# Long convolution spread over projection and FFN units, FFN units dealt out anew, some FFN weights of the third chunk kept split in HBM

## The chip, the cores and the metric

The kernel runs on 1 core of one Trainium2 chip. The metric is the device time of one launch in microseconds; three runs before the change took 2460.94 to 2464.22 us, with a median of 2463.81 us. The engines are PE (TensorE, matrix products), DVE (VectorE), ACT (ScalarE), POOL (GpSimd) and SP (SyncE, which here only issues DMAs; POOL issues some too). Each engine takes its instructions in the order in which the program holds them.

## The reference

One layer of a streaming encoder in float32, width 1024, on 2048 prompt tokens and on 8 sequences of 16 sample tokens with histories of their own:

```
u = rms_norm(x, norm_mix) @ w_in          # 2564 columns: z, xBC, dt, q, k, v, short conv, conformer
ya = SSD(z, xBC, dt)                      # 4-tap conv, silu, chunked state-space scan, gated rms norm
yb = attention(q, k, v)                   # window of 128 positions in chunks of 64, ALiBi, sinks
yc = b * conv3(c * h)
yd = silu(layer_norm(conv31(a * sigmoid(g))))     # the long convolution: 31 taps, 256 channels
x = x + concat[ya, yb, yc, yd] @ w_out
x = x + (silu(hf @ w_gate) * (hf @ w_up)) @ w_down    # hf = rms_norm(x, norm_ffn), D_FF = 2816
y = rms_norm(x, norm_final)
```

All states (SSD, convolution histories, keys and values) are outputs too.

## The kernel before, in words

**Chunks.** Tokens lie along the free axis, features along the 128 partitions. `Cfg.chunks = (2, 4, 4, 3, 3)` makes five chunks c0 to c4 of 256, 512, 512, 512 (384 of the prompt and the 128 sample tokens) and 384 columns. The FFN of c0, c1 and c2 runs by units as below; that of c3 and c4 is done in a last phase in another form (`prep`, `gate2`, `up2`, then down).

**Units.** A unit is one weight tile and its products: `proj_in` has 21 (one for each name of `W_IN_TILES`: c, h, b for the short convolution, k, v, q, B, C, dt, x, z for attention and SSD, g and a for the long convolution), `proj_out` 8, and `ffn` 22 `gate`, 22 `up_` and some `down` units. In `down(j0, n, m2)` n hidden tiles from j0 on meet two output tiles; `rounds` deals the 22 hidden tiles out, (4,4,4,4,3,3) in c0 and c1 and `rounds_last` = (4,4,4,4,1,3,2) in c2. A full unit is 24 matmuls: `group` (lines 227 to 234) multiplies a high and a low part of the weights with a high and a low part of the operand, three products for each of 8 tiles.

**Weights.** `load_w` (line 208) loads a 512 KB tile into one of two `fr` buffers from SP's queue, and `split_w` (line 199) splits it into one of three `w` buffers: ACT copies the high part (line 201), DVE subtracts it for the low part (line 181). These run ahead of their unit, as far as buffers allow. Tiles with a key can be kept: in the first three chunks a third each of the 29 projection tiles (`key % 3 == ci`) is stored to HBM in its split form (1 MB, from POOL's queue, line 222), and later chunks load that straight into a `w` buffer (line 215), without ACT and DVE.

**Order.** `weave` writes the order out: it runs a list of units, and after given units it advances side work, pieces of generators that are spread evenly from one unit to another: norms, final outputs, and `mixers(c)`, which holds attention (`attend_prompt`, `attend_sample`), SSD blocks (`ssd`), the long convolution in eight pieces of up to eight taps (`conf_conv`), and the ends (`short`, `end_conf`, `end_ssd` and the attention output), which write the eight operand tiles of `proj_out` into the pool `act`. With `early` the list has all blocks of attention and SSD first and the convolution behind; `c["blocks"]` is the number of the former. A scheduler turns the order into one instruction order per engine.

**Buffers that matter here.** `act` has 16 buffers: 8 normalised tiles for `proj_in`, 8 operand tiles for `proj_out` or the FFN (`hf`); in c3 the sample attention and SSD need four of them for caches and states. `raw` has 2: an input of a convolution with its history in front; chunk 3 also loads sample histories into it and stores new ones from it (line 390). `mix` has 4, `b2` 4, `nt` 3 (x tiles, squares). Products go to four PSUM buffers, `pm`.

**The last chunks.** After `proj_out(c2)` the units of `proj_in(c3)`, in the order `FIRST` (g and a last), are merged with c2's first 18 FFN units, and 23 more follow. Then come `proj_out(c3)`, 3 FFN units, `proj_in(c4)` merged with 5, 9 more; then `proj_out(c4)` and 6, and 8 `down` units. `norm2(c2)` makes the hf tiles near the start of c3's list, `norm1(c4)` the operands of chunk 4, `stats2` the row norms of c3 and c4 for the last phase, and `prep` its operands in four rounds. In `proj_out` of c3 and c4 an x tile is loaded (line 841), the product added, and the sum stored to `mid` (line 847).

Of the kernel before, what the change touches and what calls it, by code (L numbers as in the profile page):

```python
# [17 lines left out]
P = 128  # L18
# [22 lines left out]
FIRST = ("B", "C", "x0", "x1", "dt", "k", "v", "q0", "q1", "c0", "h0", "b0", "c1", "h1", "b1", "z0", "z1",  # L41
         "g0", "a0", "g1", "a1")

EARLY = 11
# [71 lines left out]
def stream_step(ctx: ExitStack, tc: tile.TileContext, cfg, x, w_in, w_out, w_gu, w_down, tab, con, dist_p, dist_s,  # L116
# [87 lines left out]


    kept = {}

    def load_w(src, shape, key=None, ci=0):
        n = int(np.prod(shape))
        pat = {2: lambda v: v.rearrange("p (a b) -> p a b", b=shape[-1]),  # L210
               3: lambda v: v.rearrange("p (a b c) -> p a b c", b=shape[1], c=shape[2])}[len(shape)]
        with tc.high_priority(offset=AHEAD):
            if key in kept:
                d = mk(wp, [P, 2, 1024], "w", F32R, bufs=B["w"])
                sync.dma_start(d.bitcast(F32), kept[key])
            else:
                raw = mk(wp, [P, 1024], "fr", bufs=B["fr"])
                sync.dma_start(pat(raw[:, :n]), src)
                d = split_w(raw[:, :n], n)
        if key is not None and key not in kept and key % 3 == ci:  # L220
            kept[key] = dp.tile([P, 2, 1024], F32, tag=f"kept{key}", name=f"kept{key}")
            pool.dma_start(kept[key], d.bitcast(F32))
        return pat(d[:, 0, :n]), pat(d[:, 1, :n])

    tail = [None]
# [595 lines left out]
    def proj_in(c, names):  # L821
        c.setdefault("u", {})

        def unit(name):
            wh, wl = load_w(w_in[W_IN_TILES.index(name)], [KT, P], W_IN_TILES.index(name), c["i"])
            ps = mk(pm, [P, 512], "pm")
            group(ps, c["T"], [(wh[:, k], wl[:, k], c["xn"][k]) for k in range(KT)])
            after_in(c, name, ps)
# [3 lines left out]
    def proj_out(c):  # L832
# [3 lines left out]
        def unit(m):  # L836
# [4 lines left out]
            sync.dma_start(x2[:, :T], x[:, m, o:o + T])  # L841
            wh, wl = load_w(w_out[m], [KT, P], len(W_IN_TILES) + m, c["i"])
            ps = mk(pm, [P, 512], "pm")
# [28 lines left out]
    def ffn(c):  # L872
# [5 lines left out]
        def gate(j):  # L878
            wh, wl = load_w(w_gu[j, 0], [KT, P])
            ps = mk(pm, [P, 512], "pm")  # L880
# [5 lines left out]
        def up_(j):  # L886
            wh, wl = load_w(w_gu[j, 1], [KT, P])
            ps = mk(pm, [P, 512], "pm")
# [7 lines left out]
        def down(j0, n, m2, final):  # L896
            wh, wl = load_w(w_down[:, 2 * m2:2 * m2 + 2, j0:j0 + n], [2, n, P])
            for i in range(2):
# [53 lines left out]
    def twice(g, n=2):  # L952
        return [g] * n
# [25 lines left out]
    for c, nxt, after in ((c0, c1, c2), (c1, c2, c3)):  # L979
# [6 lines left out]

    weave(proj_out(c2), (twice(final(c1)), 0, 2), (twice(norm1(c3)), 0, 3))
    f = ffn(c2)
    s3 = proj_in(c3, FIRST)
    units = s3[:3] + merge(s3[3:], f[:18]) + f[18:41]  # L990
    m3 = mixers(c3, True)
    nb = c3["blocks"]
    weave(units, (twice(norm2(c2)), 0, 2), (m3[:nb], units.index(s3[8]) + 1, units.index(s3[-1]) + 6),
          (m3[nb:], units.index(s3[-1]) + 1, len(units) - 1),
          (twice(norm1_stats(c4)), 20, 35))
    s4 = proj_in(c4, FIRST)
    units = proj_out(c3) + f[41:44] + merge(s4, f[44:49]) + f[49:58]
    m4 = mixers(c4, True)
    nb = c4["blocks"]
    weave(units, ([stats2(c3)], 8, 9), (twice(norm1(c4)), 8, 11), (m4[:nb], units.index(s4[8]) + 1, units.index(s4[-1])), (m4[nb:], units.index(s4[-1]) + 1, len(units) - 1))  # L1000

# [157 lines left out]

    weave(proj_out(c4) + f[58:64], ([stats2(c4)], 8, 9), (prepared[:2], 9, 13))  # L1160
    operands.close()
# [226 lines left out]
```

## Time and profile before

| | |
|---|---|
| time of the profiled execution, its span | 2461.09 us, 2459.3 us |
| median of three runs | 2463.81 us |
| busy: PE, DVE, ACT, POOL | 2367.5, 1589.3, 876.7, 130.8 us |
| mean granted clock of TensorE | 0.987 |
| moved by DMA | 393.77 MB, mean 160 GB/s |
| splits of weight tiles (ACT line 201, DVE line 181) | 375 each |
| loads of kept tiles, stores of them | 88, 29 |

"Busy" is the time in which an engine had at least one instruction running. Matmuls overlap, so PE's busy time holds stretches in which it runs slowly. The granted clock is the share of full speed that the chip allowed TensorE. A view by stretches gives the busy time of each engine between two moments, counted from the start of the span; a view of waits gives who waited for whom, in us in total, times, and the longest.

### The profile page before, as it was taken

How to read it: one execution, taken by the hardware profiler on the slowest of the kernel's cores; microseconds unless marked ns; L12 is line 12 of the kernel's file. 1: busy time of each engine (PE TensorE's matmuls, PEld its weight loads, DVE VectorE, ACT ScalarE, POOL GpSimd, SP SyncE). 2: the span in 40 equal slices, each digit the busy share in tenths (PEclk: the TensorE clock that was granted, in tenths of full speed). 3: DMA queues.
4: the chain of work that ended last, by engine and by line, in shares of the span. 5: the costliest groups of instructions: out<-in, count | busy, mean ns of one | idle time of the engine just before them, and what ended most of it. 6: DMA issues, size and time to landing. Idle time of an engine off the chain costs nothing.

```text
span 2459.3 us, 32394 instructions
## 1 busy us (share of the span) xinstructions
PE 2367.5 (96%) x12443; PEld 2052.3 (83%) x12443; DVE 1589.3 (65%) x2997; ACT 876.7 (36%) x1461; POOL 130.8 (5%) x240
## 2 busy tenths in 40 slices
PE   6899999999999999989999999998889999999997
PEld 5788999878888888877887788987868999999997
DVE  6897998765784546556248963558497676663324
ACT  4534455423333233224112431332244444443221
POOL 0100000010000000010000000000001000000000
PEclk9999999999999999999999999999889999999998
DMA  7657445576422222466443136643533323338663
GB/s 250 247 174 271 138 155 163 197 266 248 146 89 87 91 90 78 153 248 174 148 143 128 62 103 235 219 164 112 192 112 116 127 92 120 124 117 300 213 195 118
DMA packets 130746, 393.77 MB, mean 160 GB/s; under 512 B 12464, under 2 KB 50256, under 8 KB 115616
## 3 DMA queue, kind: packets, MB, share of 16 engines
q1 hardware_dynamic: 116560, 327.20, 40.4%
q0 software_dynamic: 14032, 64.51, 7.1%
q8 instruction: 98, 1.61, 0.3%
q14 instruction: 56, 0.46, 0.1%
HBM read 326.69 MB, written 64.97 MB: 159 GB/s over the span
## 4 chain that ended last, share of the span: by engine, by line
PE 44%; issue 6%; DVE 3%; DMA 2%; ACT 0%; POOL 0%; DVEq 0%; SPq 0%; POOLq 0%; ACTq 0%
PE pm L1102 6%; PE pm L1103 6%; PE pm L1104 6%; PE pm L231 6%; PE pm L232 6%; PE pm L233 6%; PE px L1103 1%; PE px L1102 1%; PE px L1104 1%; DMA nt<-x 1%; DVE w L181 1%; DVE x L184 0%; DMA o_xc_s<-raw 0%; DMA act<-kc 0%; PE px L655 0%
## 5 line engine op out<-in xcount | busy, mean ns | idle before, releaser
L231 PE MATMUL pm<-act,w 128*128 128x512 f32 (+2 forms) x2216 | 804.2, 364 | 16.6 <-DMA w<-kept 7.0
L233 PE MATMUL pm<-act,w 128*128 128x512 f32 (+2 forms) x2216 | 796.8, 360 | 5.2 <-DVE w L181 5.1
L232 PE MATMUL pm<-act,w 128*128 128x512 f32 (+2 forms) x2216 | 795.8, 359 | 1.4 <-DVE act L181 1.4
L201 ACT ACTIVATE w<-fr 128x1024 fp32r<-128x1024 f32 (+3 forms) x375 | 388.3, 1036 | 892.9 <-PE pm L233 524.1
L181 DVE TENSOR_TENSOR w<-fr,w 128x1024 fp32r<-128x1024 f32 (+3 forms) x375 | 448.4, 1196 | 288.3 <-ACT w L201 287.0
L231 PEld LDWEIGHTS pm<-act,w 128*128 128x128 f32 x2216 | 420.2, 190 | 85.2 <-issue 9.4
L233 PEld LDWEIGHTS pm<-act,w 128*128 128x128 f32 x2216 | 420.3, 190 | 64.6 <-DVE w L181 7.5
L232 PEld LDWEIGHTS pm<-act,w 128*128 128x128 f32 x2216 | 420.6, 190 | 59.4 <-DVE act L181 2.3
L1102 PE MATMUL pm<-hf,w 128*128 128x448 f32 x616 | 225.6, 366 | 0.8 <-ACT g L1116 0.6
L1103 PE MATMUL pm<-hf,w 128*128 128x448 f32 x616 | 224.8, 365 | 0.0
L1104 PE MATMUL pm<-hf,w 128*128 128x448 f32 x616 | 223.8, 363 | 0.0
L231 PE MATMUL pm<-h,w 128*128 128x512 f32 (+1 forms) x528 | 192.3, 365 | 19.6 <-DVE x L181 12.9
L184 DVE SCALAR_TENSOR_TENSOR mix<-raw,tabh,mix 128x384 f32<-128x384 f32 (+3 forms) x360 | 199.9, 594 | 1.8
L232 PE MATMUL pm<-h,w 128*128 128x512 f32 (+1 forms) x528 | 189.2, 359 | 0.0
L233 PE MATMUL pm<-h,w 128*128 128x512 f32 (+1 forms) x528 | 188.3, 357 | 0.0
L181 DVE TENSOR_TENSOR x<-x,pm 128x512 f32<-128x512 f32 (+2 forms) x184 | 107.6, 600 | 67.4 <-PE pm L233 55.1
L231 PEld LDWEIGHTS pm<-h,w 128*128 128x128 f32 x528 | 100.3, 190 | 41.1 <-issue 12.3
L184 DVE SCALAR_TENSOR_TENSOR ft<-ft,pm 128x512 f32<-128x512 f32 (+1 forms) x132 | 78.7, 596 | 84.2 <-PE pm L233 67.2
L1102 PEld LDWEIGHTS pm<-hf,w 128*128 128x128 f32 x616 | 115.6, 188 | 10.6 <-ACT g L1116 1.0
L1104 PEld LDWEIGHTS pm<-hf,w 128*128 128x128 f32 x616 | 115.7, 188 | 9.4
L1103 PEld LDWEIGHTS pm<-hf,w 128*128 128x128 f32 x616 | 115.7, 188 | 8.2
L233 PEld LDWEIGHTS pm<-h,w 128*128 128x128 f32 x528 | 100.4, 190 | 15.2
(283 smaller groups left out, 2572.8 us busy)
## 6 DMA issues: line engine op xcount, KB each, us to landing
w<-kept SPq DMA_DIRECT2D x88, 1024.0 KB, 5.5
fr<-w_gu SPq DMA_DIRECT2D x176, 512.0 KB, 3.3
fr<-w_down SPq DMA_DIRECT2D x92, 512.0 KB, 3.7
kept<-w POOLq DMA_DIRECT2D x29, 1024.0 KB, 6.6
fr<-w_in SPq DMA_DIRECT2D x42, 512.0 KB, 4.3
hm<-h POOLq DMA_DIRECT2D x44, 448.0 KB, 4.4
ht<-hm SPq DMA_DIRECT2D x40, 448.0 KB, 5.2
nt<-x SPq DMA_DIRECT2D x56, 256.0 KB, 5.6
```

The costliest lines, as they stand in the source:

```text
L181: return eng.tensor_tensor(out=out, in0=a, in1=b, op=op)
L184: return eng.scalar_tensor_tensor(out=out, in0=a, scalar=s, in1=b, op0=op0, op1=op1)
L201: act.activation(d[:, 0, :n], raw, AF.Copy)
L231: pe.matmul(ps[:, :T], wh, o[:, 0, :T], start=(i == 0), stop=False)
L232: pe.matmul(ps[:, :T], wh, o[:, 1, :T], start=False, stop=False)
L233: mm = pe.matmul(ps[:, :T], wl, o[:, 0, :T], start=False, stop=(i == n - 1))
L1102: pe.matmul(ps[:, :N], wh[:, i], a, start=first and i == 0, stop=False, skip_group_check=True)
L1103: pe.matmul(ps[:, :N], wh[:, i], b, start=False, stop=False, skip_group_check=True)
L1104: mm = pe.matmul(ps[:, :N], wl[:, i], a, start=False, stop=(i == n - 1), skip_group_check=True)
```

## The change

The projection tiles are stored in chunks 1 and 2 only: even ones in chunk 1, the rest in chunk 2. Half of the FFN tiles (gates with even j, ups with odd j, down tiles with even m2) are stored in chunk 1's FFN and looked up by key in chunk 2's. In c3 and c4, `proj_in` runs in the order `SPREAD`, with g0 and a0 first and g1 and a1 in the middle; the pieces of the first convolution are spread from a0 to a1, those of the second, and `short`, from a1 to eight units before the end, the attention and SSD blocks from q1 to two units behind z1, and the ends of the mixers over the last seven units. c2's FFN units are dealt out anew over the three lists, and the norms around `proj_out(c2)` and the first rounds of `prep` are spaced differently.

```diff
+SPREAD = ("g0", "a0", "B", "C", "x0", "x1", "dt", "k", "v", "q0", "q1", "g1", "a1", "c0", "h0", "b0", "c1", "h1", "b1",
+          "z0", "z1")
...
-    def load_w(src, shape, key=None, ci=0):
+    def load_w(src, shape, key=None, store=False):
...
-                sync.dma_start(d.bitcast(F32), kept[key])
+                sync.dma_start(d[:, :, :n].bitcast(F32), kept[key])
...
-        if key is not None and key not in kept and key % 3 == ci:
-            kept[key] = dp.tile([P, 2, 1024], F32, tag=f"kept{key}", name=f"kept{key}")
-            pool.dma_start(kept[key], d.bitcast(F32))
+        if store and key not in kept:
+            uid[0] += 1
+            kept[key] = dp.tile([P, 2, n], F32, tag=f"kept{uid[0]}", name=f"kept{uid[0]}")
+            pool.dma_start(kept[key], d[:, :, :n].bitcast(F32))
         return pat(d[:, 0, :n]), pat(d[:, 1, :n])
+
+    def keep(c, n):
+        return c["i"] in (1, 2) and (c["i"] == 2 or n % 2 == 0)
...
-            wh, wl = load_w(w_in[W_IN_TILES.index(name)], [KT, P], W_IN_TILES.index(name), c["i"])
+            wh, wl = load_w(w_in[W_IN_TILES.index(name)], [KT, P], W_IN_TILES.index(name), keep(c, W_IN_TILES.index(name)))
...
-            wh, wl = load_w(w_out[m], [KT, P], len(W_IN_TILES) + m, c["i"])
+            wh, wl = load_w(w_out[m], [KT, P], len(W_IN_TILES) + m, keep(c, m))
...
-            wh, wl = load_w(w_gu[j, 0], [KT, P])
+            wh, wl = load_w(w_gu[j, 0], [KT, P], ("gu", j, 0), c["i"] == 1 and j % 2 == 0)
...
-            wh, wl = load_w(w_gu[j, 1], [KT, P])
+            wh, wl = load_w(w_gu[j, 1], [KT, P], ("gu", j, 1), c["i"] == 1 and j % 2 == 1)
...
-            wh, wl = load_w(w_down[:, 2 * m2:2 * m2 + 2, j0:j0 + n], [2, n, P])
+            wh, wl = load_w(w_down[:, 2 * m2:2 * m2 + 2, j0:j0 + n], [2, n, P], ("down", m2, j0, n),
+                            c["i"] == 1 and m2 % 2 == 0)
...
-    weave(proj_out(c2), (twice(final(c1)), 0, 2), (twice(norm1(c3)), 0, 3))
+    weave(proj_out(c2), (twice(final(c1)), 0, 4), (twice(norm1(c3)), 1, 5))
     f = ffn(c2)
-    s3 = proj_in(c3, FIRST)
-    units = s3[:3] + merge(s3[3:], f[:18]) + f[18:41]
-    m3 = mixers(c3, True)
-    nb = c3["blocks"]
-    weave(units, (twice(norm2(c2)), 0, 2), (m3[:nb], units.index(s3[8]) + 1, units.index(s3[-1]) + 6),
-          (m3[nb:], units.index(s3[-1]) + 1, len(units) - 1),
-          (twice(norm1_stats(c4)), 20, 35))
-    s4 = proj_in(c4, FIRST)
-    units = proj_out(c3) + f[41:44] + merge(s4, f[44:49]) + f[49:58]
-    m4 = mixers(c4, True)
-    nb = c4["blocks"]
-    weave(units, ([stats2(c3)], 8, 9), (twice(norm1(c4)), 8, 11), (m4[:nb], units.index(s4[8]) + 1, units.index(s4[-1])), (m4[nb:], units.index(s4[-1]) + 1, len(units) - 1))
+    def beside(c, s, units, end):
+
+        st = mixers(c, True)
+        at = {n: units.index(u) + 1 for n, u in zip(SPREAD, s)}
+        n = c["blocks"]
+        assert at["z1"] <= end - 7
+        return [(st[n:n + 4], at["a0"], at["a1"] - 1), (st[:n], at["q1"], min(at["z1"] + 2, end - 8)),
+                (st[n + 4:n + 9], at["a1"], end - 8), (st[n + 9:], end - 7, end)]
+
+    s3 = proj_in(c3, SPREAD)
+    units = s3[:3] + merge(s3[3:], f[:26]) + f[26:36]
+    weave(units, (twice(norm2(c2)), 0, 2), *beside(c3, s3, units, len(units) - 1), (twice(norm1_stats(c4)), 20, 35))
+    s4 = proj_in(c4, SPREAD)
+    units = proj_out(c3) + f[36:39] + merge(s4, f[39:44]) + f[44:53]
+    weave(units, ([stats2(c3)], 8, 9), (twice(norm1(c4)), 8, 11), *beside(c4, s4, units, len(units) - 1))
...
-    weave(proj_out(c4) + f[58:64], ([stats2(c4)], 8, 9), (prepared[:2], 9, 13))
+    weave(proj_out(c4) + f[53:64], ([stats2(c4)], 8, 9), (prepared[:2], 10, 17))
```

## The prediction

> **What bounds the kernel now.** I read the page's busy line and clock line first, then the waits of PE, then the busy time stretch by stretch, with the stretches cut where the stages of the code change.
>
> ```profile
> PE 2367.5 (96%) x12443; PEld 2052.3 (83%) x12443; DVE 1589.3 (65%) x2997; ACT 876.7 (36%) x1461; POOL 130.8 (5%) x240
> PEclk9999999999999999999999999999889999999998
> ```
>
> PE is the bound nearly everywhere, and the change leaves its number of matmuls as it is. So what can be won or lost is the time in which PE stands, or runs at a lower granted clock. The digits fall to 8 in slices 29 and 30, with PE still in the nineties: that loss does not show as idle time. The stretches show where it lies (columns: length, busy of PE, weight loads, DVE, ACT, POOL with counts, granted clock, DMA share, GB/s):
>
> ```profile
> core 0: us, PE busy (x) PEld busy (x) DVE busy (x) ACT busy (x) POOL busy (x), PEclk, DMA share, GB/s
> 18.00:109.00 91.00, 77.10 (x566) 71.34 (x567) 67.96 (x158) 44.61 (x87) 8.31 (x17) 0.98 0.71 252
> 109.00:177.00 68.00, 67.95 (x326) 54.69 (x326) 64.24 (x168) 24.56 (x52) 4.37 (x6) 1.00 0.57 194
> 644.00:1035.00 391.00, 391.00 (x1819) 316.69 (x1818) 237.12 (x402) 127.35 (x209) 8.95 (x16) 1.00 0.29 92
> 1085.00:1160.00 75.00, 67.11 (x295) 54.55 (x294) 51.75 (x110) 29.20 (x51) 8.70 (x11) 0.98 0.55 154
> 1160.00:1306.00 146.00, 146.00 (x639) 119.83 (x638) 61.00 (x119) 24.26 (x33) 6.19 (x9) 1.00 0.45 149
> 1306.00:1396.00 90.00, 87.71 (x555) 67.22 (x556) 75.02 (x218) 40.40 (x95) 7.37 (x20) 0.96 0.27 89
> 1396.00:1481.00 85.00, 85.00 (x388) 69.72 (x387) 61.47 (x120) 25.52 (x36) 0.00 (x0) 1.00 0.30 99
> 1543.00:1678.00 135.00, 133.62 (x775) 121.39 (x774) 73.42 (x173) 46.32 (x104) 9.32 (x22) 1.00 0.55 188
> 1678.00:1723.00 45.00, 35.75 (x145) 28.40 (x144) 43.35 (x79) 6.57 (x10) 0.54 (x1) 0.89 0.30 103
> 1723.00:1771.00 48.00, 42.47 (x220) 40.15 (x219) 19.54 (x51) 9.73 (x18) 2.70 (x5) 0.86 0.52 189
> 1771.00:1788.50 17.50, 15.35 (x73) 12.61 (x71) 9.39 (x23) 5.42 (x8) 1.62 (x3) 0.90 0.51 173
> 1788.50:1811.00 22.50, 22.50 (x101) 18.45 (x101) 21.97 (x36) 11.82 (x20) 0.00 (x0) 1.00 0.43 132
> 1811.00:1851.00 40.00, 31.77 (x121) 24.18 (x120) 37.49 (x63) 17.22 (x30) 0.00 (x0) 0.87 0.28 87
> ```
>
> Loss of a stretch = its length minus PE busy, plus (1 − clock) × PE busy. It is 15.4 us in 18 to 109 (chunk 0's projection), 9.2 in 1085 to 1160 (start of chunk 3's), 5.8 in 1306 to 1396 (chunk 3's attention and SSD), then 13.2, 11.5, 3.7, 0 and 12.4 in the five last stretches: 40.8 us in 173 us. From 1160 to 1306 nothing is lost: 639 matmuls in 146 us are 228 ns each, so a unit of 24 matmuls over 512 columns takes 5.5 us. The change works mostly on those 40.8 us.
>
> In the last five stretches DVE is full (43.35 of 45, 21.97 of 22.5, 37.49 of 40), and the waits name it:
>
> ```profile
> PE pm L231 <- DVE x L181: 12.9, 4, 9.2
> PE pm L231 <- ACT hf L196: 4.5, 2, 4.3
> ```
>
> One wait of 9.2 us and one of 4.3 carry most of it. The DVE work in front of the first is chunk 4's long convolution (count, ns min/median/max, first and last start):
>
> ```profile
> L184 DVE SCALAR_TENSOR_TENSOR mix<-raw,tabh,mix x56: 610/617/628, 1675.0 to 1722.3; 128x384 f32<-128x384 f32 x56
> ```
>
> 56 taps, 33 us of DVE, all after the last projection unit, since g and a stand last in `FIRST`.
>
> **Part 1: the convolutions move.** With g0, a0 first, the taps lie beside projection and FFN units. Chunk 4's 33 us fit into 1543 to 1678, where DVE has 135 − 73 = 62 us free; chunk 3's go into the counterpart of 1160 to 1306, with 85 free. There they cost nothing; if DVE were full there, they would cost their own length. After the last projection unit of chunk 4 the code now has eight units of 5.5 us and one of 1.4 (45 us) for the ends of its mixers. So the 9.2 us wait and the stand at out4.0 go, with their half clock. What is late next is the chain of x tiles in proj_out(4): three `nt` buffers serve x load, add, square and store to `mid`.
>
> ```profile
> 1554.90:1571.50 16.60, 16.60 (x97) 16.60 (x96) 9.58 (x19) 4.07 (x7) 1.62 (x3) 1.00 0.57 167
> ```
>
> ```profile
> L181 DVE TENSOR_TENSOR nt<-nt,pm x8: 553/554/555, 1743.1 to 1779.8; 128x384 f32<-128x384 f32 x8
> ```
>
> Four units of chunk 4 take 16.6 us, 4.15 each. The eight adds come (1779.8 − 1743.1) / 7 = 5.24 us apart. Unhindered, PE gets ahead by 7 × 1.09 = 7.6 us, and behind out4.7 now stand three units of 1.4 us that want two PSUM tiles each, where one unit of 5.5 us wanted one. PE will stand there some 6 us and then run a while at half clock: I leave 9 us (between 4 and 15) of the 28.4 of the three stretches to 1788.5. Gain 19 (13 to 24).
>
> The Trainium skill ("TensorE: Matmul & The Clock Gate", Part 1) says that one idle window of about 3.4 us halves the clock until a busy window has passed. By that rule only the 9.2 and the 4.3 us waits would trip it, 1.7 us of loss each, and what I leave at out4 would be 7.7, the sum 1.3 us better. The rows say more: the clock columns alone are worth 3.9 + 5.9 + 1.5 + 4.1 = 15.4 us, so I price a stand with more than one window.
>
> **Part 2: preparation of the last phase.** Two of `prep`'s four rounds are due before the last eight units, two among them; its splits span both:
>
> ```profile
> L181 DVE TENSOR_TENSOR hf<-g,hf x28: 618/621/626, 1791.9 to 1841.2; 128x448 fp32r<-128x448 f32 x28
> ```
>
> Between out4.7 and those eight units there will be 3 × 1.4 + 8 × 5.5 = 48 us instead of 33, and four of the eight larger units load kept weights where all were split before, so the first two rounds are done in time. The last two still wait for the operand tiles of u2.21, and with the eight units' own work fill DVE (37.49 of 40, for units that need 27). Of 12.4 us I expect 4 to go (0 to 8).
>
> **Part 3: start of chunk 3.**
>
> ```profile
> PE px L264 <- DVE n L184: 4.4, 1, 4.4
> ```
>
> ```profile
> 1099.38 0.17 DVE L348 COPY raw<-hx 128x3 f32<-128x3 f32 x1 [4.21 <-DMA o_xc_s<-raw]
> ```
>
> ```profile
> o_xc_s<-raw POOLq DMA_DIRECT2D x4, 12.0 KB, 9.4
> ```
>
> norm2's Newton steps stood behind a copy that waited for a raw buffer whose store takes 9.4 us. With g0 and a0 ahead of B, both raw buffers are free then: 4.4 us and 1.3 of clock go. But a0 keeps one of two buffers until its fourth conv piece (unit 20), so B, C, x0, x1 share the other. C's copy comes 5.5 us after B's store and waits 9.4: DVE stands 4 us with the last hf tiles behind it, PE 0 to 6, I take 3. Net gain 3 (−1 to 6). C to x0 to x1 are 11 us or more apart.
>
> **Part 4: chunk 0 stores nothing.** Seven 1 MB stores leave 18 to 109, three leave proj_out(0).
>
> ```profile
> fr<-w_in SPq DMA_DIRECT2D x15, 512.0 KB, 4.4
> kept<-w POOLq DMA_DIRECT2D x6, 1024.0 KB, 7.2
> ```
>
> ```profile
> fr<-w_gu SPq DMA_DIRECT2D x7, 512.0 KB, 3.2
> ```
>
> ```profile
> PE pm L233 <- DVE w L181: 4.4, 7, 0.8
> ```
>
> Beside those stores a raw load takes 4.4 us (39 to 100), without them 3.2 (640 to 700), and PE waited 4.4 us for splits. Gain 3 (0 to 6).
>
> **Part 5: splits and kept loads.**
>
> ```profile
> L181 DVE TENSOR_TENSOR w<-fr,w 128x1024 fp32r<-128x1024 f32 (+3 forms) x375 | 448.4, 1196 | 288.3 <-ACT w L201 287.0
> ```
>
> ```profile
> w<-kept SPq DMA_DIRECT2D x88, 1024.0 KB, 5.5
> ```
>
> ```profile
> kept<-w POOLq DMA_DIRECT2D x29, 1024.0 KB, 6.6
> ```
>
> Projection splits go from 57 to 72: four more among chunk 1's first eleven units, where DVE has 64.24 of 68, so 4 × 1.2 = 4.8 us that may reach out0; the others where it has room. Cost 1 (0 to 5). Thirty FFN tiles of chunk 2 come split: 36 us of DVE less, but in stretches where DVE is free anyway (61 of 146), apart from those counted in part 2. Gain 0. They need 34 stores in 644 to 1035, four of which nothing reads (rounds 16–3 and 19–3 of chunk 1 are dealt 16–1, 17–3, 20–2 in chunk 2). 33 MB in 391 us are 84 GB/s on 92, a share of about 0.55; a store lands 6.6 us after issue, a unit takes 5.5, so a buffer comes free up to 1 us later, two units before it is needed. Behind a store on POOL's queue wait the SSD broadcasts, with POOL busy 9 of 391 us. A kept load takes 5.5 us, with 11 ahead on SP. Cost 0 (0 to 4).
>
> **Part 6: chunk 3's mixers have less cover.** Its sample attention needs `act` tiles, which come free after the last projection unit: now z1, 11 units (60 us) before out3.0, formerly a1, 26 units before.
>
> ```profile
> L706 PE MATMUL px<-act,qs x32: 269/293/418, 1310.2 to 1312.9; 64*32 64x128 f32 x32
> ```
>
> ```profile
> L683 PE MATMUL px<-b,vt x24: 379/379/430, 1364.3 to 1396.1; 128*64 128x256 f32 x24
> ```
>
> ```profile
> L196 ACT ACTIVATE act<-mix x2: 609/622/634, 1457.4 to 1459.7; 128x512 fp32r<-128x512 f32 x2
> L196 ACT ACTIVATE act<-xx x2: 632/632/633, 1465.9 to 1468.3; 128x512 fp32r<-128x512 f32 x2
> L196 ACT ACTIVATE act<-q x2: 615/616/616, 1468.8 to 1469.3; 128x512 fp32r<-128x512 f32 x2
> ```
>
> ```profile
> 1306.00:1396.00 90.00, 16.82 (x36) 0.96 0.27 89
> ```
>
> From the release at 1306 to the last attention matmul were 90 us; from the first to the last of the late mix tiles, 12. Cover: 60 us of units, the blocks' own PE work, 90 − 10 units × 5.5 − 5.8 = 29, and 6 of loss: 95 against 102. The last row is DVE on the convolution tiles alone: 17 us of taps that leave the blocks' 90. Cost 2 (0 to 12).
>
> Sum: 19 + 4 + 3 + 3 − 1 − 0 − 2 = 26. The profiled execution took 2461.1 us (span 2459.3), 2.7 under the runs' median of 2463.8. 2461.1 − 26 = 2435.1 on its scale, **2438** on that of the median.
>
> **Rivals.** *A, little gain (0.15):* the x chain grows longer once PE no longer waits ahead of it and keeps 15 us instead of 9, prep gives nothing instead of 4, and the shared raw buffer costs 7 instead of 3 at chunk 3's start: 26 − 6 − 4 − 4 = 12, about 2452. For it: 5.24 us against 4.15. Against: the DMA share there is only 0.52. *B, slower (0.10):* chunk 3's tail. In the trace 73 us pass between the last attention matmul (1396.1) and the last mix split (1469.3). I price the tail at 12, since much of that time was taps and the pacing by the unit order; if it is a chain of waits, out3.0 stands for it. With a stand of 26 us more than I count all gain is gone, with 40 the time is 2478, and 61 (73 − 12) is the most. For it: PE and DVE take their queues in order, so one late tile holds all. Against: DVE had 61 of the 85 us from 1396 to 1481 full of work, most of it not the tail's. *C, nothing (0.05):* DVE's order is made by a scheduler, and a copy waiting for the one raw buffer holds the taps behind it, so that they end up where they were: gains of parts 3 and 4 against 5 and 6, 2461.
>
> **How the numbers follow.** The forecast has 0.70 (own range 2429 to 2448, with parts 1 and 2 at their ends), A 0.15, B 0.10, C 0.05. The range 2421 to 2460 takes in A and leaves out B and the best ends of all terms. About 0.2% (5 us) is what measuring this kernel can tell from no change. Faster by over that: 0.69 of the forecast, 0.13 of A, 0.01 of C, together 0.83. Within: 0.01, 0.02, 0.03 of these and 0.01 of B, 0.07. Slower: 0.09 of B, 0.01 of C, 0.10.
>
> **What would show it.** Right: no wait of PE on `DVE x` over 3 us between out3 and the last eight units; the first `nt` add of chunk 4 some 5 us after out4.0 starts and the eight still 5 us apart; a stand of PE of 3 to 8 us behind out4.7; chunk 3's L264 wait gone; kept loads 103, kept stores 63, splits 360. Wrong: out3.0 waiting over 10 us for a mix tile (B); taps still running beside out4 (C); PE losing over 5 us in 109 to 260, or anything in the stretch of chunk 1's FFN.

## The result and the profile after

The changed kernel takes 2434.99 us (median of 4 runs, 2428.43 to 2442.06) where the kernel before takes 2463.18 us (4 runs, 2460.94 to 2464.22): a ratio of 0.9887, 95% interval 0.9855 to 0.9919, 28 us faster. Comparisons leave out one disturbed execution, of the run no_out_kept below (2912 us at a granted clock of 0.75). The profiled execution took 2428.43 us with a span of 2426.7: it lies at the low end, and 32.6 us of span are gained in it. Line numbers of the changed kernel are three to twelve higher than before: products 239 to 241 (231 to 233), DVE's two-tensor helper 184 (181), its multiply-add helper 187 (184).

The busy line and the clock line of the page:

```profile
PE 2355.6 (97%) x12443; PEld 2043.0 (84%) x12443; DVE 1573.4 (65%) x2982; ACT 859.9 (35%) x1446; POOL 149.4 (6%) x274
PEclk9999999999999999999999999999999999999998
```

The matmuls are the same 12443, and the two digits of 8 in slices 29 and 30 are gone. The stretches, cut where the same stages begin (columns as in the prediction: length, busy and counts of PE, weight loads, DVE, ACT, POOL, granted clock, DMA share, GB/s):

```profile
18.00:94.00 76.00, 72.70 (x567) 68.61 (x568) 67.92 (x152) 46.65 (x90) 5.87 (x11) 1.00 0.58 194
628.00:1019.00 391.00, 391.00 (x1820) 316.58 (x1819) 241.77 (x419) 128.26 (x209) 27.55 (x54) 1.00 0.52 177
1019.00:1074.50 55.50, 49.49 (x219) 40.59 (x218) 25.52 (x45) 10.10 (x14) 5.94 (x11) 0.94 0.83 311
1074.50:1182.00 107.50, 100.42 (x432) 80.25 (x431) 85.27 (x192) 34.82 (x61) 10.68 (x12) 0.98 0.56 175
1182.00:1340.00 158.00, 158.00 (x694) 129.56 (x693) 62.40 (x116) 19.57 (x29) 7.12 (x13) 1.00 0.47 163
1340.00:1442.00 102.00, 97.69 (x609) 74.56 (x609) 67.03 (x210) 41.46 (x103) 5.14 (x15) 0.95 0.31 111
1447.30:1646.50 199.20, 195.97 (x1051) 171.95 (x1049) 120.84 (x267) 53.76 (x116) 15.44 (x31) 1.00 0.63 212
1646.50:1695.40 48.90, 48.90 (x226) 40.37 (x225) 25.81 (x58) 11.42 (x21) 0.00 (x0) 1.00 0.31 107
1695.40:1753.00 57.60, 51.90 (x281) 47.70 (x280) 25.90 (x53) 11.16 (x21) 4.32 (x8) 1.00 0.74 266
1753.00:1786.00 33.00, 33.00 (x145) 27.05 (x145) 23.78 (x38) 12.14 (x19) 0.00 (x0) 1.00 0.50 177
1786.00:1818.70 32.70, 29.45 (x122) 23.73 (x121) 32.14 (x54) 16.37 (x28) 0.00 (x0) 0.95 0.25 83
```

Chunk 0's projection takes 76 us here, where the same row took 91 before (18 to 109). With the prediction's formula for the loss (idle PE plus the clock's share of busy PE), the last stages, from 1678 on before and from 1646.5 on here, lose 40.8 us before and 0 + 5.7 + 0 + 4.7 = 10.4 now. The waits of PE say what is late in the new kernel (the line waiting, what it waited for, us in total, times, longest):

```profile
PE pm L239 <- DMA w<-kept: 9.7, 5, 3.5
PE pm L239 <- DVE x L184: 6.8, 3, 6.0
...
PE px L714 <- DMA act<-kc: 4.3, 1, 4.3
...
PE pm L239 <- ACT hf L199: 3.3, 1, 3.3
```

The same three waits in the kernel before, over its whole span:

```profile
PE pm L231 <- DVE x L181: 15.0, 7, 9.2
...
PE pm L231 <- DMA w<-kept: 7.0, 7, 2.0
...
PE px L706 <- DMA act<-kc: 2.2, 1, 2.2
```

The 9.2 us wait for an x tile is gone. New is one of 6.0 us (at 1050, in the output projection of chunk 2). The wait for the sample caches (at 1347) is twice as long as before, and the waits for kept tiles are fewer and longer. The transfers and the convolution's taps:

```profile
w<-kept SPq DMA_DIRECT2D x103, 1024.0 KB, 5.3
...
kept<-w POOLq DMA_DIRECT2D x59, 1024.0 KB, 6.4
...
kept<-w POOLq DMA_DIRECT2D x4, 768.0 KB, 5.3
```

```profile
L187 DVE SCALAR_TENSOR_TENSOR mix<-raw,tabh,mix x60: 608/619/621, 1524.6 to 1617.9; 128x384 f32<-128x384 f32 x60
```

The counts are the forecast ones (103 loads, 59 + 4 stores), and chunk 4's taps, which ran from 1670 to 1722 up to the output projection, now end 77 us ahead of it.

### The profile page after: what moved, and what is told of

It reads as the page before. It is cut to its first block, busy times and chain, and to the rows that moved or that the text cites. A ratio compares the mean times of both kernels' runs of the same rounds, so it can differ in the third digit from the quotient of the medians.

```text
span 2426.7 us, 32445 instructions
## 1 busy us (share of the span) xinstructions
PE 2355.6 (97%) x12443; PEld 2043.0 (84%) x12443; DVE 1573.4 (65%) x2982; ACT 859.9 (35%) x1446; POOL 149.4 (6%) x274
## 4 chain that ended last, share of the span: by engine, by line
PE 68%; issue 16%; DVE 7%; DMA 6%; ACT 2%; POOL 1%; SPq 0%; DVEq 0%; POOLq 0%; ACTq 0%
PE pm L239 13%; PE pm L240 13%; PE pm L241 13%; PE pm L1114 7%; PE pm L1115 7%; PE pm L1116 7%; DVE mix L187 2%; DVE w L184 2%; DMA nt<-x 2%; PE px L1116 1%; PE px L1115 1%; PE px L1114 1%; DMA fr<-w_in 1%; DMA w<-kept 1%; ACT w L204 1%
## 5 line engine op out<-in xcount | busy, mean ns | idle before, releaser
L204 ACT ACTIVATE w<-fr 128x1024 fp32r<-128x1024 f32 (+3 forms) x360 | 372.4, 1035 | 843.5 <-PE pm L241 476.6
L184 DVE TENSOR_TENSOR w<-fr,w 128x1024 fp32r<-128x1024 f32 (+3 forms) x360 | 429.6, 1194 | 274.6 <-ACT w L204 271.9
```

What stands on the lines that cost most here:

```text
L184: return eng.tensor_tensor(out=out, in0=a, in1=b, op=op)
L204: act.activation(d[:, 0, :n], raw, AF.Copy)
```

## The experiments

The change and the twelve runs, as ratios to the kernel before, which ran beside each group of them on the same chip (medians of 2463.2 to 2465.4 us, so 0.001 is 2.5 us):

| run | ratio, 95% interval |
|---|---|
| the change (first comparison) | 0.9887 (0.9855 to 0.9919) |
| after_again | 0.9894 (0.9876 to 0.9911) |
| keep_part | 0.9967 (0.9955 to 0.9980) |
| order_part | 0.9907 (0.9894 to 0.9921) |
| no_ffn_kept | 0.9869 (0.9849 to 0.9889) |
| dummy_store | 0.9940 (0.9917 to 0.9964) |
| c4_back | 0.9876 (0.9855 to 0.9896) |
| c3_back | 0.9908 (0.9890 to 0.9925) |
| out2_back | 0.9880 (0.9862 to 0.9898) |
| sample_last | 0.9847 (0.9827 to 0.9866) |
| no_out_kept | 0.9801 (0.9783 to 0.9820) |
| both | 0.9801 (0.9779 to 0.9823) |
| late | 0.9771 (0.9751 to 0.9790) |

**The change in two halves.** `keep_part` is the kernel before with the new `load_w`, `keep` and keys; `order_part` is the changed kernel with the old ones.

```diff
 # keep_part, on the kernel before
-            wh, wl = load_w(w_out[m], [KT, P], len(W_IN_TILES) + m, c["i"])
+            wh, wl = load_w(w_out[m], [KT, P], len(W_IN_TILES) + m, keep(c, m))
 ...
 # order_part, on the changed kernel
-            wh, wl = load_w(w_out[m], [KT, P], len(W_IN_TILES) + m, keep(c, m))
+            wh, wl = load_w(w_out[m], [KT, P], len(W_IN_TILES) + m, c["i"])
 ...
```

> The order of the units and of the mixers is that of the kernel before; only the rule for kept weights is the changed one (chunk 0 stores nothing, chunks 1 and 2 store, half the FFN tiles of chunk 1 are kept for chunk 2). Theory 1, the forecast's terms: chunk 0's stores are worth 3 us, the four more splits among chunk 1's first units cost 1, kept FFN tiles give nothing: 2 us faster than before, about 2461. Theory 2, from the two traces, where chunk 0's stage ends 15 us earlier (3 of them at its very start): the stores alone are worth 11 us, the splits cost 1.5, and kept tiles among the last downs give up to 5 us more: about 2453 without that, 2448 with it. Stage marks: under theory 1 chunk 0's last projection unit ends at about 103 us, under theory 2 at 94 to 97.

> The order of the units and of the mixers is the changed one; the rule for kept weights is that of the kernel before (chunk 0 stores its third, no FFN tile is kept). Theory 1, the forecast's terms: convolutions 19, preparation 4, chunk 3's start 3, less 2 for chunk 3's cover: 24 us faster than before, about 2439. Theory 2, from the traces: 19 for the convolutions of chunk 4, less 6 for a new stand in the last output projection before chunk 3, less 4 in chunk 3, plus 0 to 8 in the last eight units (8 if the order alone gives it, 0 if the kept FFN tiles do): 9 to 17 us faster, 2446 to 2454. If the two parts are independent, this gain and that of the rule alone add up to 28.

The rule alone gives 8 us, the order alone 23; together 31, against 28 measured (26 the second time). The order is worth what the forecast gave it, 24. The rule is worth more than theory 1's 2 (5 to 11 by its interval) and at best the least that theory 2 allowed, 10; its trace says why. Chunk 0's stretch, and below it the one of chunk 2's output projection:

```profile
18.00:94.50 76.50, 72.31 (x569) 67.74 (x570) 68.45 (x152) 47.32 (x90) 5.01 (x11) 1.00 0.60 196
```

```profile
1024.10:1077.30 53.20, 47.44 (x218) 38.32 (x216) 32.15 (x55) 14.00 (x21) 5.94 (x11) 1.00 0.89 330
```

Chunk 1's first unit starts at 94.5 as in the changed kernel, 109.3 before: theory 2's 15 us are there. But later stages take most of it back. The same output projection in the kernel before:

```profile
1035.30:1084.70 49.40, 47.21 (x217) 38.59 (x217) 29.68 (x52) 12.44 (x19) 5.42 (x10) 1.00 0.89 321
```

It loses 5.8 us where it lost 2.2, with two waits for kept tiles of 4.3 us together, and chunk 3's stage, up to its output projection, takes 401.0 us where it took 396.7. Of the 15 us the span of this trace keeps 3.6, and the runs' times keep 8. That the stores, which moved from chunk 0 to chunks 1 and 2, are what takes it back is likely; below, taking some of them away is tested.

**Why chunk 0's stores cost 15 us.** The changed kernel, with stores added that hold no buffer and wait for nothing:

```diff
+        if dummy:
+            for q in range(4):
+                uid[0] += 1
+                dump = dp.tile([P, 512], F32, tag=f"dump{uid[0]}", name=f"dump{uid[0]}")
+                pool.dma_start(dump, cn[:, :512])
 ...                                        # dummy is set for the ten tiles that chunk 0 stored before
```

> The changed kernel with stores added that nothing reads: for the seven projection tiles and three output tiles of chunk 0 that the kernel before stored, 1 MB each (four DMAs of 256 KB on the same queue) goes to HBM from a table that is never written again, so that no weight buffer is held and the queue never waits for a split. The question is why chunk 0's stores cost 15 us and not the 3 of the forecast. Theory 1, the transfers: they slow the raw loads that chunk 0's units wait for, so the stage from the second unit to the end of chunk 0's projection loses 24 us again (before 25.5, changed 13.6) and the whole is 8 to 15 us slower than the changed kernel, 2443 to 2450. Theory 2, the held buffers: a weight buffer that is being stored is free 7 us later, and GpSimd's queue stands until the split is done; without that the stage stays at 14 to 16 and the whole at 2435 to 2437.

```profile
18.00:108.60 90.60, 78.64 (x568) 74.01 (x569) 68.48 (x152) 48.25 (x91) 19.50 (x38) 0.94 0.76 266
```

Chunk 0 ends at 108.6 us again, though this trace is of the slowest of the six executions (2460.48 us, the median is 2447.90). Over the runs the whole loses 11 us against after_again (0.9940 and 0.9894). So the transfers alone bring back most of the 15 us, and theory 2, by which nothing would come back, falls; whether held buffers add something is not separated. The times to landing of the raw loads between chunk 0's second unit and its end (min, median, max), in the kernel before, in the change and with the added stores:

```profile
DMA to landing us min/median/max: 3.1/4.4/7.8
```

```profile
DMA to landing us min/median/max: 3.1/3.6/4.8
```

```profile
DMA to landing us min/median/max: 3.2/4.2/8.6
```

With stores beside them the median rises by less than 1 us, but the slowest load takes 7.8 or 8.6 us instead of 4.8; the mean DMA share of 0.71 did not tell that. In this stretch ACT waits 18.9 us for raw loads in the kernel before and 7.7 in the change. With the added stores it waits 8.3 for them and 6.1 for a tile of x, and the granted clock is 0.94. So slow loads fit the delay, but by which wait it reaches PE differs between the two and is not settled.

**The convolutions' place.** The changed kernel, with the same units per stage, but chunk 4's part of the order put back:

```diff
-    s4 = proj_in(c4, SPREAD)
+    s4 = proj_in(c4, FIRST)
     units = proj_out(c3) + f[36:39] + merge(s4, f[39:44]) + f[44:53]
-    weave(units, ([stats2(c3)], 8, 9), (twice(norm1(c4)), 8, 11), *beside(c4, s4, units, len(units) - 1))
+    m4 = mixers(c4, True)
+    nb = c4["blocks"]
+    weave(units, ([stats2(c3)], 8, 9), (twice(norm1(c4)), 8, 11), (m4[:nb], units.index(s4[8]) + 1, units.index(s4[-1])),
+          (m4[nb:], units.index(s4[-1]) + 1, len(units) - 1))
```

> The changed kernel, with the same units in each stage, but with chunk 4's projection in the order of before (g and a last) and its mixers' items placed as before: the convolutions of chunk 4 stand behind its last projection unit again. Theory 1, part 1 of the forecast: the 9.2 us wait for an x tile and the stand at the first output unit come back, 13 to 24 us slower than the changed kernel, 2448 to 2459, nearest to 2454; chunk 4's stage and its output projection are 19 us longer in the trace, and 56 taps run in the last 50 us before the output projection. Theory 2, the stands were due to the short last FFN units dealt to that place and not to the taps: with the new deal most of the gain stays, 2435 to 2442.

> The changed kernel once more, beside the others on one chip. Its four runs so far lay between 2428 and 2442. If they scatter by chance of the transfers, this gives 2430 to 2440 again with a spread of about 14 us, and a ratio of 0.986 to 0.990; the marks of the stages show which stages differ from one execution to another.

c4_back is not slower at all: theory 1, the main step of my forecast, falls, and theory 2's time holds. Its taps, its longest waits of PE from 1480 on, then its stages (from the first unit of chunk 3's output projection; from the last unit of chunk 4's input projection; from its output projection; two more):

```profile
L187 DVE SCALAR_TENSOR_TENSOR mix<-raw,tabh,mix x60: 609/614/620, 1635.2 to 1684.6; 128x384 f32<-128x384 f32 x60
```

```profile
PE pm L239 <- DVE nt L184: 3.5, 1, 3.5
PE pm L239 <- ACT hf L199: 3.3, 1, 3.3
PE pm L239 <- ACT act L199: 2.4, 1, 2.4
```

```profile
1449.20:1643.80 194.60, 194.56 (x1050) 172.15 (x1049) 92.44 (x213) 54.75 (x119) 14.02 (x30) 1.00 0.66 217
1643.80:1691.50 47.70, 47.61 (x213) 38.76 (x213) 43.65 (x78) 6.94 (x10) 0.54 (x1) 1.00 0.33 118
1691.50:1760.80 69.30, 59.17 (x293) 53.72 (x292) 34.42 (x86) 14.54 (x28) 4.34 (x8) 0.90 0.60 217
1760.80:1793.80 33.00, 33.00 (x146) 27.06 (x145) 23.72 (x38) 12.09 (x19) 0.00 (x0) 1.00 0.52 177
1793.80:1824.90 31.10, 27.84 (x121) 22.25 (x119) 30.59 (x51) 15.16 (x26) 0.00 (x0) 1.00 0.28 87
```

The same stages of after_again, the first three:

```profile
1448.00:1650.00 202.00, 198.09 (x1048) 173.57 (x1048) 120.45 (x266) 53.21 (x116) 15.44 (x31) 0.98 0.62 209
1650.00:1699.40 49.40, 49.40 (x231) 40.48 (x228) 26.23 (x58) 11.89 (x23) 0.00 (x0) 1.00 0.31 106
1699.40:1760.50 61.10, 54.99 (x281) 50.46 (x280) 26.01 (x53) 11.19 (x21) 4.32 (x8) 0.94 0.69 250
```

The taps are back behind the last projection unit, and the 9.2 us wait for an x tile is not. In c4_back DVE is as full behind the last projection unit as before (43.65 of 47.7 us, 43.35 of 45 before), and PE loses only 0.1 us there: eight of the nine units beside the taps are long ones of 5.5 us, where before four of the nine were short ones of 1.4 us. Only at the output projection it loses 10.1 + 5.9 = 16.0 us. With the convolutions spread, that is 5.7 (the change) or 9.4 (again), but chunk 4's projection, which lost 0.0, loses 3.2 or 7.9. The longest waits of PE in that stage of the change are:

```profile
PE px L531 <- ACT ut L522: 1.9, 1, 1.9
PE pm L241 <- DVE w L184: 1.0, 1, 1.0
```

The second is for a split. The first is for ACT's copy of v, and ACT had stood 6.4 us in front of it for `xx`, the 4-tap convolution of SSD's x: on DVE its taps alternate with those of the long convolution, from 1541 to 1557. The first of these stages before:

```profile
1481.40:1678.00 196.60, 195.22 (x1051) 172.22 (x1050) 97.53 (x217) 59.51 (x124) 13.68 (x30) 1.00 0.59 200
```

From the output projection of chunk 3 to the last eight units the loss is 29.8 before (1.4 here and 28.4 from 1678 to 1811, as in the prediction), 16.2 with the new deal alone, and 8.9 or 17.3 with the convolutions moved as well. So with the new deal, moving chunk 4's convolutions is worth nothing that can be measured in the runs' times (0.9887 and 0.9894 with them moved, 0.9876 without). What c4_back shares with the change in this stretch is the deal and the rule for kept tiles. The rule alone gives nothing there: by the starts of units keep_part takes 328.5 us for the stretch, the kernel before 329.1. So the 13.6 us go with the deal. No run has the old deal with the convolutions moved, so whether moving them would have won as much there is open.

`c3_back` comes from the other side: on the kernel out2_back (below), chunk 3's stage is as before, with 41 FFN units, so that chunk 4's spread has 12 FFN units where the change has 17.

```diff
+    s3 = proj_in(c3, FIRST)
+    units = s3[:3] + merge(s3[3:], f[:18]) + f[18:41]
 ...
-    units = proj_out(c3) + f[36:39] + merge(s4, f[39:44]) + f[44:53]
+    units = proj_out(c3) + f[41:43] + merge(s4, f[43:45]) + f[45:53]
```

> The order of the output projection of chunk 2 and the whole of chunk 3's stage (unit order, mixers, 41 FFN units) are as before; chunk 4's stage has the changed unit order and places, with 12 FFN units beside and behind its projection where the change has 17; the last stage is the changed one, and so is the rule for kept weights. Theory 1, the forecast's terms: parts 3 and 6 together are worth 1 us, so this is 1 us slower than with the change there, about 2435, and chunk 4's gain of 19 us stays. Theory 2, from the trace: chunk 3's stage takes 59 to 61 us over its matmuls with the change and 57 before, so putting it back gives 1 to 4 us: 2430 to 2433. Rival: with five FFN units fewer beside chunk 4, its taps and blocks no longer fit (VectorE had 104 of 146 us there) and 5 us or more of chunk 4's gain go: over 2438.

```profile
1516.50:1656.30 139.80, 130.47 (x739) 117.02 (x737) 99.17 (x237) 42.35 (x99) 12.42 (x24) 0.96 0.62 197
```

```profile
PE px L531 <- ACT ut L522: 5.2, 1, 5.2
PE pm L239 <- ACT act L199: 2.3, 1, 2.3
```

The rival is right about the time: it is 7 us slower than out2_back (0.9908 against 0.9880, whose intervals just overlap). Chunk 4's projection with its 99 us of DVE in 140 loses 9.3 + 5.2 = 14.5 us, so 40 free us of DVE did not hide the taps. The longest wait is again the one for ACT's copy of v. ACT stood 3.7 us for `xx`, whose taps alternate with the long convolution's, and DVE itself stood twice, 2.5 and 2.3 us, for a `raw` buffer whose store had not landed. DVE has such stands in c4_back too (12.0 us in four) and PE doesn't wait there, so the alternating taps are the likely cause; no run isolates them.

**Kept FFN tiles.**

```diff
-            wh, wl = load_w(w_gu[j, 0], [KT, P], ("gu", j, 0), c["i"] == 1 and j % 2 == 0)
+            wh, wl = load_w(w_gu[j, 0], [KT, P])
 ...
```

> The changed kernel, without any FFN tile kept (no FFN stores in chunk 1, every FFN tile of chunk 2 loaded and split). Theory 1, the forecast: the kept FFN tiles cost and give nothing but part of the 4 us of the preparation: 2435 to 2438, the same as the changed kernel within noise, and nothing changes in the stretch of chunk 1's FFN. Theory 2: the 7.6 us that the last eight units won come from the kept tiles there, and the splits come back beside chunk 4's convolutions: 2440 to 2447. Rival: the 34 stores cost time in chunk 1's FFN or make the runs scatter: faster than the changed kernel, under 2432.

The ratio is 0.9869 against 0.9887 and 0.9894, with intervals that overlap: the kept FFN tiles give nothing, as the forecast had it, or a little less than nothing. Theory 2 is out. By the starts of units the last eight take 32.6 us without kept FFN tiles, as in the change; order_part has 32.5, keep_part 39.9 and the kernel before 40.2. So the order gives this gain; its parts there (the first rounds of `prep` earlier, more units ahead) were not tested one by one.

**The new stand in chunk 2's output projection.**

```diff
-    weave(proj_out(c2), (twice(final(c1)), 0, 4), (twice(norm1(c3)), 1, 5))
+    weave(proj_out(c2), (twice(final(c1)), 0, 2), (twice(norm1(c3)), 0, 3))
```

> The changed kernel with one line of the order put back: in the output projection of chunk 2, final(c1) is due between units 0 and 2 and norm1(c3) between 0 and 3, as before (the change made them 0 to 4 and 1 to 5). The forecast gave this line no term: 0, so 2435. The trace shows a new wait of PE of 6.0 us there for an x tile, since VectorE stood 9.9 us in front of a product of final(c1) that PE has in its queue behind a whole unit: if that is a price of this line, 5 to 6 us faster than the changed kernel, about 2429.5, and the 6.0 us wait is gone. Rival: with the order put back the stand moves to chunk 3's first units, whose norm comes later than it could: 2435 again, with a wait of PE of 4 us or more at chunk 3's first units.

The 6.0 us wait goes, but the time does not move measurably. Of the 9.0 us that the stage loses in the change, 5.6 stay (53.0 us, PE busy 47.37), and the waits now read:

```profile
PE pm L239 <- DMA w<-kept: 4.0, 2, 2.2
PE pm L239 <- DVE x L184: 1.7, 1, 1.7
```

Behind the one wait stood another, for kept tiles. Four stores and four loads of 1 MB lie in that stage (DMA share 0.89). The share alone does not explain it: the kernel before has 0.89 there too, with two such stores and six such loads, and loses 2.2 us. The next run, on the kernel out2_back, takes the kept tiles of the output projections away.

```diff
-            wh, wl = load_w(w_out[m], [KT, P], len(W_IN_TILES) + m, keep(c, m))
+            wh, wl = load_w(w_out[m], [KT, P])
```

> The changed kernel with the order of the output projection of chunk 2 put back, and without any kept weight for the output projections: each of their tiles is loaded at 0.5 MB and split, where stores of 1 MB (4 in chunk 1, 4 in chunk 2) and kept loads of 1 MB (4 in chunk 2, 8 in chunk 3, 8 in chunk 4) stood. Theory 1, transfers bind there (DMA share 0.83 beside the output projections of chunks 2 and 4, PE waits 4.0 and 4.8 us for kept tiles in them): those waits go, 4 to 8 us faster, 2426 to 2430 against 2433.7 without this edit. Theory 2, the chain of x tiles through the DMA queue and the three nt buffers binds, whatever the weights come from: same within 2 us. Rival: 20 more splits of 1.2 us on VectorE and 1.1 on ScalarE stand ahead of the adds: slower, by up to 5 us.

```profile
1024.40:1072.30 47.90, 46.91 (x217) 38.66 (x216) 34.12 (x56) 16.21 (x23) 4.35 (x8) 1.00 0.72 250
1695.70:1729.00 33.30, 33.30 (x194) 33.30 (x193) 17.33 (x25) 10.72 (x16) 3.79 (x7) 1.00 0.64 204
```

Theory 1 comes nearest, and the gain is more than it said: 0.9801 against 0.9880, some 19 us. Chunk 2's output projection loses 1.0 us, chunk 4's nothing in 33.3 us where the change needs 34.8. There DVE and ACT have room for the splits (17 and 11 of 33 us), and the DMA share is 0.64 where the change has 0.79. By the starts of units in the two traces chunk 2's output projection is 5.1 us shorter than in out2_back and the way from chunk 4's to the last eight units 6.2. But what lies between them is 7.5 us longer, and the two spans are only 2 us apart (2421.8 and 2423.9): out2_back's trace is of the fastest of its four executions, no_out_kept's of the slowest of the five that were compared. So the 19 us stand in the runs' times, and the traces do not place them. Nor does a run tell here whether the bytes cost or the `w` buffers that a store holds.

**Chunk 3's sample items.** The base of `sample_last` is the changed kernel with out2_back's line; `both` has the edit of no_out_kept as well.

```diff
-        if c["Ts"]:
-            def load_h0(): ...
-            add((once(load_h0), 1))
-            add((attend_sample(c), 3), (ssd(c, c["Tp"], True), 2))
 ...                                        # the same lines now follow the loop over the prompt blocks
```

> The changed kernel with the order of the output projection of chunk 2 put back, and in the mixers of chunk 3 the items on the sample rows (load of the states, sample attention, sample SSD) stand behind the three prompt blocks and no longer ahead of them. Nothing is left out. In the changed kernel the sample items need operand tiles that come free only with chunk 3's last projection unit, and the prompt blocks queue behind them: PE loses 14 us from 1320 to 1440. Theory 1, the held items are the cause: the prompt blocks run beside the projection, only the sample block is left for the late stretch, 5 to 10 us are won: 2424 to 2429 against 2433.7 without this edit, and the loss of that stretch falls below 8 us. Theory 2, the loss is the sample block itself (its caches land late, its chain through PE, VectorE and ScalarE is serial): it moves to just before out3.0 and that waits: 2433 to 2440.

> The changed kernel with three edits: the order of the output projection of chunk 2 put back, the sample items of chunk 3 behind its prompt blocks, and no kept weights for the output projections. If the first theories of the two runs with one of these edits hold, their gains add up: 9 to 18 us against 2433.7, that is 2416 to 2425, faster than the changed kernel by 0.4 to 0.8 per cent. If the held items and the transfers are not what costs, the same as 2434 or slower.

The prompt blocks do run beside the projection now (the products of line 691 from 1240 to 1325 instead of 1399 to 1427), and the time is 0.9847, 8 us better than out2_back, as theory 1 of `sample_last` had it. But PE still stands 4.5 us for the caches, and the stretch from 1320 on still loses 4.5 + 4.7 = 9.2 us, not under 8, so the wait for the caches remains most of the loss there. Added to no_out_kept the edit gives nothing that can be measured (`both`, 0.9801), and why the two gains do not add up is open. The last run, on the kernel `both`, places the products on the caches two units later:

```diff
+        if c["Ts"]:
+            p = n - 6
+            return [(st[n:n + 4], at["v"], at["a1"] - 1), (st[:p], at["q1"], at["z1"]),
+                    (st[n + 4:n + 9], at["a1"], end - 8), (st[p:n], end - 8, end - 5), (st[n + 9:], end - 5, end + 1)]
```

> The kernel with the three edits (output projection of chunk 2 in its order of before, sample items of chunk 3 behind its prompt blocks, no kept weights for the output projections), and two more places in chunk 3 changed: the six sample items are due from two units behind the last projection unit on, the ends one or two units later, and the first four pieces of the convolution from v on instead of from a0 on. Theory 1: PE stood 5.4 us for the sample caches because its products were queued right behind the unit that frees their tiles, so two units in between hide the load and the loss from 1320 to 1440 falls from 13 us to under 7; and PE stood 4.0 and 1.8 us around 1130 to 1180 because taps filled VectorE there ahead of the splits, so that goes too: together 6 to 11 us faster than 2415, 2404 to 2409. Theory 2: the sample block's chain is then the last thing ahead of chunk 3's output projection, and its first unit waits 5 us or more: 2415 or slower; and the kept loads around 1150 are late of themselves, so that the wait for them stays.

The late stretch of `both`, then that of `late`:

```profile
1313.00:1435.00 122.00, 116.59 (x626) 94.12 (x625) 61.00 (x143) 29.86 (x56) 4.80 (x11) 0.94 0.38 133
```

```profile
1320.00:1430.00 110.00, 110.00 (x636) 88.93 (x635) 60.83 (x152) 33.34 (x62) 5.79 (x12) 1.00 0.43 151
```

5.4 + 7.0 = 12.4 us of loss are gone, and chunk 3's output projection starts without a wait: for the sample items theory 1 holds. For the kept tiles theory 2 holds: the waits for them around 1120 stay (4.1 us). With 0.9771 (2407.56 us, median of 5 runs) this version is 56 us faster than the kernel before and some 29 faster than the change. Against `both` the gain is 7 us, hardly more than its uncertainty, and the two spans are 2407.1 (`both`) and 2408.7 (`late`), since other stretches of that trace are longer.

## Why the prediction was right, and where only its sum was

The time was forecast at 2438 (2421 to 2460) and is 2435. Point by point, on the profiled execution (32.6 us of span gained):

| step | forecast | measured |
|---|---|---|
| 1 convolutions, chunk 4 up to the last eight units | +19 | +20.9 (29.8 to 8.9 of loss); +12.5 in after_again |
| 2 last eight units | +4 | +7.7 (12.4 to 4.7) |
| 3 start of chunk 3 | +3 | 0 (9.2 to 9.1) |
| 4 chunk 0's stores | +3 | +15.1 (chunk 1's first unit 109.3 to 94.2) |
| 5 splits of chunk 1's first units; kept FFN tiles | −1; 0 | −1.5 (15.1 to 13.6 at chunk 0's output projection); 0 |
| 6 chunk 3's mixers | −2 | −3.4 (5.8 to 9.2) |
| not in the forecast: chunk 2's output projection | | −6.8 (2.2 to 9.0) |

The rows add up to 32.0. This trace is of the fastest of the four executions. So the sum of 26 came out near the median's 28 partly by luck, because errors cancelled: step 4 was put at a fifth of its size, a loss of 7 us was overlooked, and the step that carried most was near in its amount (20.9 in one trace, 12.5 in the other) and wrong in its cause.

**Step 1.** It booked the end of the 9.2 us wait on the moved taps; in c4_back the taps are back and that wait is not. "There they cost nothing" failed too: chunk 4's projection loses 3.2 or 7.9 us with the taps in it and nothing in c4_back. The signs I named all came: no wait on an x tile over 0.3 us there, the first add 4.4 us after the output projection starts, the eight 5.8 us apart, a stand of 4.4 us behind its last unit. They fit the deal as well as the taps, so they could not tell one from the other. c4_back could. The text even counted the eight long units now behind the last projection unit, and booked the gain on the other edit. The stand behind the last output unit was not PSUM tiles either: 3.5 us of it was a kept tile.

**Step 4.** I priced the stores by the median landing (4.4 against 3.2 us) and by PE's waits for splits (4.4 us). The slowest landings, which the prediction did not price, grew far more than the median, and ACT's 18.9 us of waits for raw loads stood in the trace before. dummy_store shows that the transfers cost most of it, and not by which wait. **Step 3.** The wait of 4.4 us at line 264 went, and waits for kept tiles (4.9 us) took its place. **Step 5** held to half a microsecond: chunk 1's FFN stretch is 391.0 us with PE busy throughout, before and after, with 34 stores added. **Step 6** and rival B: chunk 3's output projection did start without a wait.

**What was overlooked.** Two numbers in a line of the order, 0 to 4 for 0 to 2. DVE stood 9.9 us in its queue for a small product of `final(c1)` that PE had behind a whole unit, and the adds of the output projection stood behind it. Putting the two numbers back ends this stand, but not most of the loss of the stage, as out2_back shows. I had asked that question, who is queued behind a waiting instruction, of the waits that the diff added openly, and not of this one.

**What stays open.** The way from chunk 1's first projection unit to the first `down` unit of its FFN takes 594 to 601 us in traces of kernels with hardly any difference up to there, for no reason that I could find, and the runs of one kernel lie up to 16 us apart. From chunk 3's output projection to the last eight units, c4_back takes 344.6 us; the seven traces with both convolutions moved and the changed deal and kept projection tiles there lie between 336.1 and 345.5, around 340. So in the traces moving chunk 4's convolutions may win some 5 us, and the runs' times do not show it.

## What to carry to other kernels

A sum that comes out right does not prove its terms: undo one edit at a time, above all the one that was to carry the gain, since two edits of one diff (where work is put, and how much other work is dealt beside it) can leave the same marks in a trace. In these runs the free time of an engine did not tell whether side work is hidden: 43.65 of 47.7 us of DVE beside long units cost PE 0.1 us, and 99 of 140 us with fewer of them cost 14.5. And before keeping a derived tile in HBM, look at the stage that will load and store it: in the output projections, where the DMA share was 0.8 to 0.9, splitting the tiles again was some 19 us cheaper; for the FFN tiles it made no difference.

## What the runs showed of the hardware

A stand of PE costs its length and sometimes a lower clock after it, and the same stand does so in one execution and not in another. The last eight units hold one stand of 3.25 us in all twelve traces with the new order. In the 8 us behind it the granted clock is 0.79 in ten of them and 1.00 in two, out2_back and c4_back. The 8 us in the change and in c4_back:

```profile
1808.60:1816.60 8.00, 7.95 (x28) 6.41 (x29) 7.99 (x13) 3.48 (x5) 0.00 (x0) 0.79 0.12 46
```

```profile
1816.30:1824.30 8.00, 7.88 (x35) 6.49 (x35) 8.00 (x13) 3.37 (x5) 0.00 (x0) 1.00 0.12 45
```

These are 28 matmuls at a clock of 0.79 in the one and 35 at 1.00 in the other, a difference of 1.7 us. The Trainium skill ("TensorE: Matmul & The Clock Gate", Part 1) says that activity is watched in a free-running window of about 3.4 us, and that one kernel's count of slow matmuls varies with its phase. The traces agree that the same stand comes out differently from one execution to another. They do not bear out the length as a bound: the clock is at 0.79 behind a stand of 2.3 us (`late`, at 1120), clearly shorter than such a window, and at 1.00 behind one of 3.5 (the change, at 1739) and one of 2.2 (`both`, at 1113).
